# The first SwiGLU products of a decoder trunk: another order of the seven products, and weight sums made earlier

## The chip, the cores and the metric

The kernel runs on one core of one Trainium2 chip. The metric is the time of one execution in microseconds (us). The engines have short names: PE is TensorE (PEld its weight loader), DVE is VectorE, ACT is ScalarE, POOL is GpSimd, SP is SyncE, which issues DMAs.

## What is computed

Two layers of a decoder trunk on 512 tokens of width 1024. Each has a SwiGLU block, a mixer and a second SwiGLU block, each followed by a layer norm:

```python
def swiglu(x, w13, w2):
    a, b = jnp.split(x @ w13, 2, axis=-1)
    return (jax.nn.silu(a) * b) @ w2
...
    for l in range(DEPTH):
        x = layer_norm(ALPHA * x + 0.5 * swiglu(x, ffn1_w13[l], ffn1_w2[l]), ln_g[l, 0], ln_b[l, 0])
        m = mixer(x, w_in[l], ...)
        x = layer_norm(ALPHA * x + m, ln_g[l, 1], ln_b[l, 1])
        x = layer_norm(ALPHA * x + 0.5 * swiglu(x, ffn2_w13[l], ffn2_w2[l]), ln_g[l, 2], ln_b[l, 2])
```

The inner width of a SwiGLU is 2816, so `w13` has 22 column blocks of 128 for `a` and 22 for `b`. All data are float32. The change touches only `x @ w13`, in the four SwiGLU blocks.

## The kernel before

**Split numbers.** A float32 operand is split into a high and a low part (`split`, L126 and L127): ScalarE copies the source into a reduced type (`h_...`, the high part), and VectorE subtracts that copy from the source (`l_...`, the low part). A product is then three matmuls: high by high, high by low, low by high. So each split is a ScalarE instruction followed by a VectorE instruction that waits for it.

**Seven products instead of eight.** In `seven_pairs` two column blocks `k` and `k + 11` are taken together; with `a` and `b` that gives a two-by-two block product of the weights' quarters with the quarters of `x`. It is computed with seven products instead of eight, in which sums of quarters take the place of quarters. There are ten such pairs in a SwiGLU block (an eleventh is computed plainly first). The weights' quarters of a pair are four tiles `a`, `b`, `c`, `d` of 128x1024, loaded by SyncE (`load`, L553); four sums are made of them in place on VectorE (`sum`, L570): `t = a + b`, `b = d + b`, `a = a + b` (with the new `b`), `c = a + c` (with the new `a`). The sums of `x` are `s1` to `s4`.

**The order of the work** is written out by hand. The table `ORDER` has a row for each of the seven products: the bank of PSUM that it is added up in (`X`, `A`, or `C`, which is two banks wide), the part of `x`, and the weight tile:

```python
    ORDER = (("X", "A11", "a"), ("C", "s1", "t"), ("X", "s2", "a"), ("C", "s4", "d"), ("X", "s3", "b"),
             ("A", "A12", "c"), ("X", "A22", "c"))
    AHEAD = 3
```

The loop over `n` makes one product a step (`m` is the step in the pair, 0 to 6). In each step it issues, in this order: the evictions of the product before (`evictions`), a weight sum in the steps that have one, the split of the weights that are needed `AHEAD` = 3 steps later, and the product itself (`product` L603; `wide` L589 and L591 for bank C). The evictions bring a product out of PSUM: copies and Silu on ScalarE, adds and multiplications on VectorE. A tile that is used raw first and as a sum later (`a` is used in products one and three, `c` in six and seven) is split, summed, and split again.

In six of the ten pairs (`due`: pairs 1, 2, 4, 5, 7 and 8) the loop also calls `activation_sums` (L337 to L341, and splits) for an earlier pair's result, which the output product needs later; in three of them two DMAs (L348) then store the result.

What runs on VectorE, ScalarE and SyncE in this stage is kept in program order (`pin`). TensorE's instructions are ordered by the scheduler: it puts some matmuls of the next pair's first product ahead of this pair's last ones, since they go to another bank. POOL meanwhile adds up weight sums of the output product in DRAM by DMA (L307).

The buffers: four of `a` and `b` (two pairs' worth), two each of `c` and `d`, one of `t`, and five pairs of high and low parts. A load waits until the last reader of its buffer is done.

Of the kernel before, what the change touches and what calls it, by code (L numbers as in the profile page):

```python
# [31 lines left out]
AF = mybir.ActivationFunctionType  # L32
ALU = mybir.AluOpType
# [50 lines left out]
def trunk(ctx: ExitStack, tc, x_in, xt_in, w13, w2, w_in, w_iv, w_br, w_out, ln_g, ln_b, lb_in, hgn, sgg, sgb, sgws,  # L84
          sgbs, masks, tril_in, ident_in, out):
    nc = tc.nc
    V, S, G, PE = nc.vector, nc.scalar, nc.gpsimd, nc.tensor
# [9 lines left out]
    def bank(name):  # L97
        return psum.tile([P, 512], F32, tag="ps", name=name)
# [21 lines left out]
    def pin(ins):  # L120

        if pinned[0]:
            tc.keep_in_program_order(ins)

    def split(hi, lo, src):
        pin(S.activation(hi, src, AF.Copy))  # L126
        pin(V.tensor_tensor(lo, src, hi.bitcast(F32), op=ALU.subtract))  # L127
# [371 lines left out]
    def x_sums(s, gap=X_GAP):  # L499
# [26 lines left out]
        for q in range(2):  # L526
# [2 lines left out]
        parts("s4")  # L529


    ORDER = (("X", "A11", "a"), ("C", "s1", "t"), ("X", "s2", "a"), ("C", "s4", "d"), ("X", "s3", "b"),
             ("A", "A12", "c"), ("X", "A22", "c"))
    AHEAD = 3

    class PairWeights:
# [25 lines left out]
        def split(self):  # L562
            src = ORDER[len(self.parts)][2]
            hi, lo = (wk.tile([P, 2, 512], F32R, tag="w", name=f"{v}_p{src}_{self.k}", bufs=NW) for v in "hl")
# [7 lines left out]
    def seven_pairs(seven, s, ks, weights_of, first, due):  # L572


        half = slice(0, 256), slice(256, 512)
        movs = {"A11": lambda m: (xh[m // 2][:, m % 2, half[0]], xl[m // 2][:, m % 2, half[0]]),
                "A12": lambda m: (xh[2 + m // 2][:, m % 2, half[0]], xl[2 + m // 2][:, m % 2, half[0]]),
                "A22": lambda m: (xh[2 + m // 2][:, m % 2, half[1]], xl[2 + m // 2][:, m % 2, half[1]])}
        for c in s:
            movs[c] = lambda m, c=c: tuple(s[c][m // 2][:, m % 2, z] for z in range(2))  # L580

        def wide(ps, units, c, first):

            for z in range(2):
                hi, lo = units[0][:, z], units[1][:, z]
                for m in range(4):
                    ms = slice(m * P, (m + 1) * P)
                    v = s[c][m // 2][:, m % 2]
                    PE.matmul(ps[z][:, 0:256], lo[:, ms], v[:, 0], start=first and m == 0, stop=False,  # L589
                              skip_group_check=True)  # L590
                    PE.matmul(ps[z], hi[:, ms], v.rearrange("p z t -> p (z t)"), start=False, stop=(m == 3),  # L591
                              skip_group_check=True)
                    flow.tick(120.0 + 227.0)

        def product(ps, units, c, first):
            for z in range(2):
                hi, lo = units[0][:, z], units[1][:, z]
                for m in range(4):
                    ms = slice(m * P, (m + 1) * P)
                    mh, ml = movs[c](m)  # L600
                    for i, (a, v) in enumerate(((hi, mh), (hi, ml), (lo, mh))):
                        start = first and z == 0 and m == 0 and i == 0
                        PE.matmul(ps[:, half[z]], a[:, ms], v, start=start, stop=(m == 3 and i == 2),  # L603
                                  skip_group_check=not (first and z == 0))
                    flow.tick(3 * 120.0)

        pws = {ks[0]: first}
        at = lambda n: (ks[n // 7], n % 7)
        last = 7 * len(ks)
        banks = {}  # L610

        def evictions(k, m):

            b, r = banks[k], seven.room(k)
            X, C, A = b["X"].rearrange("p (z t) -> p z t", z=2), b["C"], b["A"].rearrange("p (z t) -> p z t", z=2)
            c12, c22 = r[:, 0:2], r[:, 2:4]
            if m == 0:
                b["c11"] = wk.tile([P, 2, 256], F32, tag="sa", name="c11", bufs=NSA)
                pin(S.activation(b["c11"], X, AF.Copy))  # L619
            elif m == 1:  # L620
                for z in range(2):
                    pin(S.activation(c22[:, z], C[z][:, 256:512], AF.Copy))
                for z in range(2):
                    pin(V.tensor_tensor(c22[:, z], c22[:, z], C[z][:, 0:256], op=ALU.add))
            elif m == 2:
                pin(S.activation(c12, X, AF.Copy))
            elif m == 3:
                for z in range(2):
                    for y in range(2):
                        pin(V.tensor_tensor(c12[:, y], C[y][:, 256 * z:256 * z + 256], c12[:, y],  # L630
                                            op=ALU.add if z else ALU.subtract))
            elif m == 4:
                pin(V.tensor_tensor(c22, c22, X, op=ALU.subtract))
            elif m == 5:
                pin(V.tensor_tensor(b["c11"], b["c11"], A, op=ALU.add))
                yield
                pin(S.activation(b["c11"], b["c11"], AF.Silu))
                pin(V.tensor_tensor(c12, c12, b["c11"], op=ALU.mult))
            elif m == 6:
                c21 = wk.tile([P, 2, 256], F32, tag="sa", name="c21", bufs=NSA)  # L640
                pin(S.activation(c21, X, AF.Silu))
                yield
                pin(V.tensor_tensor(c22, c22, c21, op=ALU.mult))

        for n in range(last):
            k, m = at(n)
            nk = at(n + 7)[0] if n + 7 < last else None
            if m == 0 and nk is not None:
                pws[nk] = weights_of(nk)
                pws[nk].load_d()  # L650
            elif m == 1 and nk is not None:
                pws[nk].load_c()
            ev = evictions(*at(n - 1)) if n else iter(())
            next(ev, None)
            if m == 0:
                banks[k] = {"X": bank(f"fX{k}"), "C": [bank(f"fC{k}{z}") for z in range(2)], "A": bank(f"fA{k}")}
            elif m == 3:
                pws[k].sum("c", "a", "c")
            elif m == 4 and nk is not None:
                pws[nk].sum("t", "a", "b")  # L660
            elif m == 5 and nk is not None:
                pws[nk].sum("b", "d", "b")
            elif m == 6 and nk is not None:
                pws[nk].sum("a", "a", "b")
            if n + AHEAD < last:
                pws[at(n + AHEAD)[0]].split()
            for _ in ev:
                pass
            if m == 3:
                for v in due.get(k, ()):  # L670
                    seven.activation_sums(v)
            c, mov, _ = ORDER[m]
            (wide if c == "C" else product)(banks[k][c], pws[k].parts[m], mov, m in (0, 1, 5))
        for _ in evictions(*at(last - 1)):
            pass

# [7 lines left out]
    def ffn(l, i, first, next_weights):  # L684
# [82 lines left out]
        in_dram = flow.add(seven.sums_in_dram(order))  # L767
        pinned[0] = True
        seven_pairs(seven, s, by_seven, weights_of, pw, dict(zip((1, 2, 4, 5, 7, 8), ([v] for v in front + by_seven[0:5]))))
        pinned[0] = False  # L770
        flow.finish(in_dram)
# [538 lines left out]
```

## Time and profile before

| | us |
|---|---|
| three runs | 2087.88, 2093.77, 2092.84 (median 2092.84) |
| the profiled execution | 2091.45 |
| its span, from the first to the last instruction | 2089.7 |
| the four stages of `seven_pairs`, from their first to their last matmul | 213.2, 216.7, 215.6, 216.6 |

The stages take 862 us together, about two fifths of the span. The profile names an instruction by its line, engine, operation and tiles: `l_pa<-ra,h_pa` is the low part of `a`'s split, made from the raw tile `ra` and the high part `h_pa`. `fX`, `fA` and `fC` are the banks, `xh` and `xl` the parts of `x`, `xs` the split sums of `x`, `r` the result of a pair, `c` at L637 or L641 the tiles `c11` and `c21`. In rows of time the first number is the start in us from the span's start, the second the duration; in square brackets stands how long the engine was idle before, and for whom. Instructions of one engine overlap a little: the time from start to start is shorter than the duration.

### The profile page before, as it was taken

How to read it: one execution, taken by the hardware profiler on the slowest of the kernel's cores; microseconds unless marked ns; L12 is line 12 of the kernel's file. 1: busy time of each engine (PE TensorE's matmuls, PEld its weight loads, DVE VectorE, ACT ScalarE, POOL GpSimd, SP SyncE). 2: the span in 40 equal slices, each digit the busy share in tenths (PEclk: the TensorE clock that was granted, in tenths of full speed). 3: DMA queues.
4: the chain of work that ended last, by engine and by line, in shares of the span. 5: the costliest groups of instructions: out<-in, count | busy, mean ns of one | idle time of the engine just before them, and what ended most of it. 6: DMA issues, size and time to landing. Idle time of an engine off the chain costs nothing. (4 is left out here: it accounts for less than half of the span.)

```text
span 2089.7 us, 32071 instructions
## 1 busy us (share of the span) xinstructions
PE 2035.9 (97%) x12240; PEld 1818.3 (87%) x12240; DVE 1645.0 (79%) x2573; ACT 1010.5 (48%) x1518; POOL 336.3 (16%) x478
## 2 busy tenths in 40 slices
PE   9999999999999999999999999999999999999998
PEld 8889888888888989998899898888888889899886
DVE  8888988956446788889788889889564468888896
ACT  5545565335323545456554455653353235444563
POOL 1322002301000122200113310032010001232001
PEclk9999999999999999999999999999999999999999
DMA  7998676735243399867669986776352434998573
GB/s 244 253 258 205 215 249 226 167 111 172 91 141 112 136 262 232 210 192 261 208 173 244 256 205 211 258 243 132 123 170 84 154 105 144 268 234 229 167 264 132
DMA packets 167546, 404.52 MB, mean 194 GB/s; under 512 B 18880, under 2 KB 19008, under 8 KB 167392
## 3 DMA queue, kind: packets, MB, share of 16 engines
q1 hardware_dynamic: 113472, 261.22, 37.3%
q0 software_dynamic: 53920, 141.26, 28.2%
q8 instruction: 96, 1.57, 0.3%
q14 instruction: 58, 0.48, 0.1%
HBM read 380.38 MB, written 131.07 MB: 245 GB/s over the span
## 5 line engine op out<-in xcount | busy, mean ns | idle before, releaser
L307 POOL DMA_DIRECT2D t<-in_w_dram x176 | 145.3, 892 | 195.4 <-DMA t<-in_w_dram 102.6
L126 ACT ACTIVATE h_pa<-ra 128x1024 fp32r<-128x1024 f32 x80 | 84.1, 1052 | 181.6 <-DVE ra L570 181.6
L127 DVE TENSOR_TENSOR l_pc<-rc,h_pc 128x1024 fp32r<-128x1024 f32 x80 | 97.9, 1224 | 47.2 <-ACT h_pc L126 47.2
L127 DVE TENSOR_TENSOR l_pa<-ra,h_pa 128x1024 fp32r<-128x1024 f32 x80 | 97.8, 1223 | 43.4 <-ACT h_pa L126 43.4
L603 PE MATMUL fX<-xh,l_pa 128*128 128x256 f32 x320 | 93.7, 293 | 38.5 <-DVE l_pa L127 38.5
L603 PE MATMUL fX<-xs,h_pa 128*128 128x256 f32 x640 | 117.1, 283 | 1.6 <-ACT c L619 1.6
L603 PE MATMUL fX<-xs,h_pb 128*128 128x256 f32 x640 | 116.7, 283 | 0.0
L591 PE MATMUL fC<-xs,h_pd 128*128 128x512 f32 x320 | 115.0, 399 | 0.0
L591 PE MATMUL fC<-xs,h_pt 128*128 128x512 f32 x320 | 114.7, 398 | 0.0
L126 ACT ACTIVATE h_pc<-rc 128x1024 fp32r<-128x1024 f32 x80 | 85.2, 1065 | 50.1 <-DVE rc L570 50.1
L603 PEld LDWEIGHTS fX<-xs,h_pa 128*128 128x128 f32 x640 | 102.0, 191 | 4.2 <-ACT c L619 2.6
L603 PEld LDWEIGHTS fX<-xs,h_pb 128*128 128x128 f32 x640 | 102.3, 191 | 2.1
L307 POOL DMA_DIRECT2D t<-t x104 | 56.4, 542 | 292.1 <-DMA t<-in_w_dram 259.7
L155 PE MATMUL z<-xh,h_z 128*128 128x512 f32 x256 | 103.1, 403 | 0.0
L155 PE MATMUL z<-xh,l_z 128*128 128x512 f32 x256 | 99.9, 390 | 0.0
L155 PE MATMUL z<-xl,h_z 128*128 128x512 f32 x256 | 99.8, 390 | 0.0
L603 PEld LDWEIGHTS fX<-xh,l_pa 128*128 128x128 f32 x320 | 61.8, 193 | 43.3 <-DVE l_pa L127 43.3
L603 PE MATMUL fX<-xh,h_pc 128*128 128x256 f32 x320 | 94.7, 296 | 0.0
L603 PE MATMUL fX<-xh,l_pc 128*128 128x256 f32 x320 | 94.6, 296 | 0.0
L603 PE MATMUL fX<-xl,h_pc 128*128 128x256 f32 x320 | 94.5, 295 | 0.0
L589 PE MATMUL fC<-xs,l_pt 128*128 128x256 f32 x320 | 90.2, 282 | 1.5 <-DVE l_pt L127 1.5
L603 PE MATMUL fX<-xl,h_pa 128*128 128x256 f32 x320 | 91.4, 286 | 0.0
(391 smaller groups left out, 6970.6 us busy)
## 6 DMA issues: line engine op xcount, KB each, us to landing
t<-in_w_dram POOLq DMA_DIRECT2D x88, 512.0 KB, 10.1
t<-t POOLq DMA_DIRECT2D x104, 256.0 KB, 5.0
r_d<-t SPq DMA_DIRECT2D x104, 256.0 KB, 4.0
t<-in_w_dram POOLq DMA_DIRECT2D x88, 256.0 KB, 6.5
r_c<-in_w_dram SPq DMA_DIRECT2D x44, 512.0 KB, 4.9
ra<-in_w_dram SPq DMA_DIRECT2D x80, 256.0 KB, 6.3
rb<-in_w_dram SPq DMA_DIRECT2D x80, 256.0 KB, 7.6
rc<-in_w_dram SPq DMA_DIRECT2D x80, 256.0 KB, 10.3
```

The costliest lines, as they stand in the source:

```text
L126: pin(S.activation(hi, src, AF.Copy))
L127: pin(V.tensor_tensor(lo, src, hi.bitcast(F32), op=ALU.subtract))
L155: PE.matmul(ps[:, n0:n0 + n], a[:, cs], m[:, n0:n0 + n], start=(i == 0), stop=(i == 3 * nk - 1))
L307: tc.keep_in_program_order(nc.gpsimd.dma_start(*of(k), **kw))
L589: PE.matmul(ps[z][:, 0:256], lo[:, ms], v[:, 0], start=first and m == 0, stop=False, skip_group_check=True)
L591: PE.matmul(ps[z], hi[:, ms], v.rearrange("p z t -> p (z t)"), start=False, stop=(m == 3), skip_group_check=True)
L603: PE.matmul(ps[:, half[z]], a[:, ms], v, start=start, stop=(m == 3 and i == 2), skip_group_check=not (first and z == 0))
```

## The change

The diff has three parts. `ORDER` is permuted: the product with `A12` and raw `c` (bank A) goes from sixth to second place, the one with `s1` and `t` (bank C) from second to fourth, the one with `s4` and `d` (bank C) from fourth to sixth; products one, three, five and seven stay. The evictions are renumbered accordingly, and the final multiplication of `c12` now follows the second product out of bank C. The sums are made in other steps, and behind the step's split and evictions instead of ahead of the split. The activation sums go from step 3 to step 1.

```diff
-    ORDER = (("X", "A11", "a"), ("C", "s1", "t"), ("X", "s2", "a"), ("C", "s4", "d"), ("X", "s3", "b"),
-             ("A", "A12", "c"), ("X", "A22", "c"))
+    ORDER = (("X", "A11", "a"), ("A", "A12", "c"), ("X", "s2", "a"), ("C", "s1", "t"), ("X", "s3", "b"),
+             ("C", "s4", "d"), ("X", "A22", "c"))
...
             elif m == 1:
+                pin(V.tensor_tensor(b["c11"], b["c11"], A, op=ALU.add))
+                yield
+                pin(S.activation(b["c11"], b["c11"], AF.Silu))
+            elif m == 2:
+                pin(S.activation(c12, X, AF.Copy))
+            elif m == 3:
                 for z in range(2):
                     pin(S.activation(c22[:, z], C[z][:, 256:512], AF.Copy))
                 for z in range(2):
                     pin(V.tensor_tensor(c22[:, z], c22[:, z], C[z][:, 0:256], op=ALU.add))
-            elif m == 2:
-                pin(S.activation(c12, X, AF.Copy))
-            elif m == 3:
+            elif m == 4:
+                pin(V.tensor_tensor(c22, c22, X, op=ALU.subtract))
+            elif m == 5:
                 for z in range(2):
                     for y in range(2):
                         pin(V.tensor_tensor(c12[:, y], C[y][:, 256 * z:256 * z + 256], c12[:, y],
                                             op=ALU.add if z else ALU.subtract))
-            elif m == 4:
-                pin(V.tensor_tensor(c22, c22, X, op=ALU.subtract))
-            elif m == 5:
-                pin(V.tensor_tensor(b["c11"], b["c11"], A, op=ALU.add))
-                yield
-                pin(S.activation(b["c11"], b["c11"], AF.Silu))
                 pin(V.tensor_tensor(c12, c12, b["c11"], op=ALU.mult))
...
-            elif m == 3:
-                pws[k].sum("c", "a", "c")
-            elif m == 4 and nk is not None:
-                pws[nk].sum("t", "a", "b")
-            elif m == 5 and nk is not None:
-                pws[nk].sum("b", "d", "b")
-            elif m == 6 and nk is not None:
-                pws[nk].sum("a", "a", "b")
             if n + AHEAD < last:
                 pws[at(n + AHEAD)[0]].split()
             for _ in ev:
                 pass
-            if m == 3:
+            if m == 0:
+                pws[k].sum("c", "a", "c")
+            elif m == 3 and nk is not None:
+                pws[nk].sum("t", "a", "b")
+            elif m == 4 and nk is not None:
+                pws[nk].sum("b", "d", "b")
+            elif m == 5 and nk is not None:
+                pws[nk].sum("a", "a", "b")
+            if m == 1:
                 for v in due.get(k, ()):
                     seven.activation_sums(v)
             c, mov, _ = ORDER[m]
-            (wide if c == "C" else product)(banks[k][c], pws[k].parts[m], mov, m in (0, 1, 5))
+            (wide if c == "C" else product)(banks[k][c], pws[k].parts[m], mov, m in (0, 1, 3))
```

No instruction is added or taken away; what moves is seen in the engines' rows. VectorE in the kernel before, from the third pair's sum `ra` to its sum `rc` (L570 are the sums, L127 the subtractions of the splits, the rest are evictions):

```order
L570 TENSOR_TENSOR ra_578<-ra_578,rb_579 128x1024
L127 TENSOR_TENSOR l_pa_791<-ra_578,h_pa_790 128x1024
L638 TENSOR_TENSOR r_627<-r_627,c_628 128x512
L127 TENSOR_TENSOR l_pd_836<-rd_584,h_pd_835 128x1024
L643 TENSOR_TENSOR r_627<-r_627,c_829 128x512
L127 TENSOR_TENSOR l_pb_870<-rb_579,h_pb_869 128x1024
L624 TENSOR_TENSOR r_866<-r_866,fC_832 128x256
L624 TENSOR_TENSOR r_866<-r_866,fC_833 128x256
L127 TENSOR_TENSOR l_pc_897<-rc_259,h_pc_896 128x1024
L570 TENSOR_TENSOR rc_259<-ra_578,rc_259 128x1024
L127 TENSOR_TENSOR l_pc_927<-rc_259,h_pc_926 128x1024
```

The same sums of the same pair on VectorE in the changed kernel:

```order
L570 TENSOR_TENSOR ra_578<-ra_578,rb_579 128x1024
L636 TENSOR_TENSOR r_628<-fC_590,r_628 128x256
L636 TENSOR_TENSOR r_628<-fC_591,r_628 128x256
L636 TENSOR_TENSOR r_628<-fC_590,r_628 128x256
L636 TENSOR_TENSOR r_628<-fC_591,r_628 128x256
L638 TENSOR_TENSOR r_628<-r_628,c_629 128x512
L127 TENSOR_TENSOR l_pa_793<-ra_578,h_pa_792 128x1024
L127 TENSOR_TENSOR l_pt_836<-rt,h_pt_835 128x1024
L643 TENSOR_TENSOR r_628<-r_628,c_829 128x512
L570 TENSOR_TENSOR rc_259<-ra_578,rc_259 128x1024
L127 TENSOR_TENSOR l_pb_871<-rb_579,h_pb_870 128x1024
```

Before, the subtraction `l_pa` and the second `l_pc` stand right behind the sums `ra` and `rc` that they read; now five evictions stand between `ra` and `l_pa`, and the second `l_pc` has moved out of the piece, to two steps later.

ScalarE in the kernel before, from the third pair's first split of `c` on (`r<-fX` is the copy `c12` out of bank X, `th` belongs to the activation sums):

```order
L126 ACTIVATE h_pc_896<-rc_259 128x1024
L626 ACTIVATE r_866<-fX_831 128x512
L126 ACTIVATE h_pc_926<-rc_259 128x1024
L126 ACTIVATE th_931<-r_400 128x256
L126 ACTIVATE th_931<-s_930 128x512
L126 ACTIVATE h_pa_965<-ra_820 128x1024
```

ScalarE in the changed kernel, from the third pair's activation sums to the copies out of bank C (L623 is the Silu of `c11`, L625 the copy `c12`):

```order
L126 ACTIVATE th_875<-r_401 128x256
L126 ACTIVATE th_875<-s_874 128x512
L126 ACTIVATE h_pd_913<-rd_584 128x1024
L623 ACTIVATE c_868<-c_868 128x512
L625 ACTIVATE r_867<-fX_831 128x512
L126 ACTIVATE h_pc_943<-rc_259 128x1024
L628 ACTIVATE r_867<-fC_832 128x256
L628 ACTIVATE r_867<-fC_833 128x256
```

The Silu of `c11`, which stood near the pair's end, now stands behind the activation sums and ahead of the copy `c12`, the split of `c` and the copies out of bank C. On SyncE the loads keep their order in the stage; at its end three loads of `r_b` (L378) have moved ahead of six fetches of stored activation sums (L356). POOL's instructions keep their order.

## The prediction

> **What bounds the kernel now.** I read the clock and span first, then the busy shares, then who waits for whom on TensorE, then the order of time on TensorE and VectorE inside the stage that the change touches.
>
> ```profile
> core 0: 2089.7 us, clock 0.993
> PE 2035.9 (97%) x12240; PEld 1818.3 (87%) x12240; DVE 1645.0 (79%) x2573; ACT 1010.5 (48%) x1518; POOL 336.3 (16%) x478
> ```
>
> TensorE works nearly all the time, so only two things can get shorter: its idle time and its slowed time. Its waits, and those of its weight loader, name the place:
>
> ```profile
> PE fX L603 <- DVE l_pa L127: 38.5, 24, 2.0
> PE pA L366 <- DVE l_b L127: 1.0, 2, 0.7
> ...
> PEld fX L603 <- DVE l_pa L127: 43.3, 24, 2.2
> ```
>
> The columns are the total in us, the number of waits and the longest one. Nearly all idle time is one kind: a product of the first SwiGLU stage waits for the low part `l_pa` of a weight that VectorE is still subtracting. There are 24 such waits: four feed-forward stages with six pairs each. In the code `due` names exactly six pairs (1, 2, 4, 5, 7, 8) in which VectorE also makes activation sums; I call them loaded pairs. TensorE in order of time, first the start of the second product in three pairs that follow each other, then one wait:
>
> ```profile
> 73.90 0.28 PE L589 MATMUL fC<-xs,l_pt 128*128 128x256 f32 x1
> ...
> 96.17 0.28 PE L589 MATMUL fC<-xs,l_pt 128*128 128x256 f32 x1
> ...
> 116.22 0.28 PE L589 MATMUL fC<-xs,l_pt 128*128 128x256 f32 x1
> ```
>
> ```profile
> 88.31 0.28 PE L603 MATMUL fX<-xl,h_pa 128*128 128x256 f32 x1
> 90.55 0.39 PE L603 MATMUL fX<-xh,l_pa 128*128 128x256 f32 x1 [1.96 <-DVE l_pa L127]
> 90.77 0.28 PE L603 MATMUL fX<-xh,h_pa 128*128 128x256 f32 x1
> 90.89 0.28 PE L603 MATMUL fX<-xl,h_pa 128*128 128x256 f32 x1
> ```
>
> A pair without a wait takes 116.22 - 96.17 = 20.05 us, which is TensorE's own work; the pair before took 22.27. Matmuls start every 0.12 us, so the gap of 2.24 us cost about 2.1. The same stretch on VectorE shows why:
>
> ```profile
> 71.61 1.22 DVE L570 TENSOR_TENSOR ra<-ra,rb 128x1024 f32<-128x1024 f32 x1
> 74.04 1.23 DVE L127 TENSOR_TENSOR l_pa<-ra,h_pa 128x1024 fp32r<-128x1024 f32 x1 [1.21 <-ACT h_pa L126]
> 75.19 0.69 DVE L638 TENSOR_TENSOR r<-r,c 128x512 f32<-128x512 f32 x1
> 76.00 1.23 DVE L127 TENSOR_TENSOR l_pd<-rd,h_pd 128x1024 fp32r<-128x1024 f32 x1
> ...
> 79.53 1.22 DVE L127 TENSOR_TENSOR l_pc<-rc,h_pc 128x1024 fp32r<-128x1024 f32 x1
> 80.79 1.23 DVE L570 TENSOR_TENSOR rc<-ra,rc 128x1024 f32<-128x1024 f32 x1
> 83.14 1.23 DVE L127 TENSOR_TENSOR l_pc<-rc,h_pc 128x1024 fp32r<-128x1024 f32 x1 [1.13 <-ACT h_pc L126]
> 84.28 0.42 DVE L337 TENSOR_TENSOR s<-r 128x256 f32<-128x256 f32 x1
> ...
> 86.81 1.41 DVE L630 TENSOR_TENSOR r<-fC,r 128x256 f32<-128x256 f32 x4
> 88.14 1.22 DVE L570 TENSOR_TENSOR rt<-ra,rb 128x1024 f32<-128x1024 f32 x1
> 89.27 1.22 DVE L127 TENSOR_TENSOR l_pa<-ra,h_pa 128x1024 fp32r<-128x1024 f32 x1
> ...
> 93.87 1.22 DVE L570 TENSOR_TENSOR ra<-ra,rb 128x1024 f32<-128x1024 f32 x1
> ...
> 113.60 1.22 DVE L570 TENSOR_TENSOR ra<-ra,rb 128x1024 f32<-128x1024 f32 x1
> ```
>
> From `ra` to `ra` VectorE needs 93.87 - 71.61 = 22.26 us in a loaded pair and 113.60 - 93.87 = 19.73 in the next. The loaded pair is VectorE's length, not TensorE's: **VectorE sets the pace there**. Twice in a pair it stands still, because it makes a weight sum and the very next thing is to split that sum: ScalarE must first copy it, and VectorE waits (1.21 and 1.13).
>
> The slowed time stands in the same stages. The first and the last of seven stretches that the trace shows at half clock, each 3.41 us long (the next to last column is the DMA share, the one before it the granted clock), and TensorE at the first:
>
> ```profile
> 781.65:785.06 3.41, 3.41 (x18) 3.41 (x17) 3.41 (x5) 0.00 (x0) 0.56 (x1) 0.50 1.10 228
> ...
> 1952.42:1955.83 3.41, 3.41 (x18) 3.41 (x17) 3.03 (x4) 0.27 (x1) 0.00 (x0) 0.50 0.42 129
> ```
>
> ```profile
> 779.10 0.28 PE L603 MATMUL fX<-xl,h_pa 128*128 128x256 f32 x1
> 781.34 0.39 PE L603 MATMUL fX<-xh,l_pa 128*128 128x256 f32 x1 [1.96 <-DVE l_pa L127]
> ...
> 781.69 0.41 PE L603 MATMUL fX<-xl,h_pa 128*128 128x256 f32 x1
> 781.90 0.41 PE L603 MATMUL fX<-xh,l_pa 128*128 128x256 f32 x1
> ```
>
> A wait ends at 781.34, and at 781.65 the clock is 0.50 for 3.41 us. Matmuls then start every 0.21 us instead of 0.12, so 3.41 / 0.21 = 16 start in the stretch, and it costs 3.41 - 16 x 0.12 = 1.5 us.
>
> The Trainium skill ("TensorE: Matmul & The Clock Gate", Part 1: The HAM clock gate) says that the gate falls back to half after at least one idle window of about 3.4 us. A gap of 2.24 us fills no such window, so by that rule the waits would not be what halves the clock, the stretches would stay and the sum would be 2052; the trace speaks against it, as the drop stands right behind the gap.
>
> **The change part by part.**
>
> *What goes.* Both standstills go: the sum `ra` now stands five VectorE instructions ahead of its split, and `rc` three products ahead. If VectorE keeps up, all 24 waits go. The loader's row is nearest to the loss: 43.3 us, plus 24 x 0.07 because a load lasts 0.19 and the next starts after 0.12 (the matmul's 0.28 against 0.12, on 38.5, gives 42.4): **45.0 us**. With the waits I let the seven half-clock stretches go: 7 x 1.5 = 10.4. Together 55.4.
>
> *What VectorE needs now.* No instruction is added or taken away, so I add up starts from the rows. Seven subtractions at 1.14 (89.27 is such a one) are 7.97; four sums at 1.13 (88.14 to 89.27) 4.53; four 512-wide evictions at 0.60 are 2.40; six 256-wide ones at 0.33 (86.81 to 88.14 for four) 2.0; activation sums 86.81 - 84.28 = 2.53. That is 19.4. It agrees with before: 22.26 less 1.30 and 1.22 (the two standstills over a start-to-start of 1.13), 0.21 before `l_pd` and 0.12 before `rc` is 19.41.
>
> *The wait that is added.* `c11` is now finished in the third step instead of the seventh. ScalarE's order there becomes Silu of `c11`, copy of `c12`, copy `h_pc`; the first waits for VectorE's add, and VectorE's `l_pc` waits for the third. Behind that Silu are queued the copy that frees bank X for the fifth product, `h_pc`, and the two copies out of bank C. The pieces:
>
> ```profile
> 72.95 1.06 ACT L126 ACTIVATE h_pa<-ra 128x1024 fp32r<-128x1024 f32 x1 [4.70 <-DVE ra L570]
> 73.92 0.61 ACT L637 ACTIVATE c<-c 128x512 f32<-128x512 f32 x1
> 74.44 0.58 ACT L641 ACTIVATE c<-fX 128x512 f32<-128x512 f32 x1
> 74.91 1.05 ACT L126 ACTIVATE h_pd<-rd 128x1024 fp32r<-128x1024 f32 x1
> ```
>
> VectorE's add 0.69, Silu 0.52, copy 0.47 (starts), `h_pc` 1.06 whole: 2.74, and 0.1 for the handings-over (71.61 + 1.22 to 72.95 is 0.12). In that time VectorE does the add's 0.60 and `l_pd`'s 1.14. So it stands 1.1 us, in every pair. Bounds: nothing, if the add comes early enough, and 2.5, the two standstills of before again. I take 1.1, a sum of rows of the same instructions.
>
> So a loaded pair costs VectorE 19.4 + 1.1 = 20.5, against TensorE's 20.05: 0.45 too much, at most 24 x 0.45 = 10.8 us of waits that stay. A pair without activation sums costs it 20.5 - 2.53 = 18.0; three pairs together, 18.0 + 2 x 20.5 = 59.0, fit into 3 x 20.05 = 60.15. Only how far VectorE can run ahead decides. It cannot evict a product before TensorE has made it, so its lead is a step (2.88) less the evictions themselves, more than one loaded pair's 0.45 and perhaps less than what two need together with the start of the stage. Ends 0 and 10.8; I take the middle, **5.4**.
>
> *The moved evictions.* Bank C is written by products four and six, bank X by one, three, five and seven; one step of 2.88 us stands between, as before. Two copies (at most 0.47 each, the start of the wider one above) and two adds (0.33 each) must empty C in it: 1.6 us hide behind product five. If VectorE is late, the wait shows there, on the sixth product. I price it within the 0 to 10.8.
>
> *The moved DMAs.* SyncE's loads follow when buffers come free. `a` comes free three steps earlier, `b` when it did, `d` two steps later, and the two stores of the activation sums, which stand between them on SyncE, go two steps earlier. The tight one is `c`: its first split is now for the second product, not the sixth, four steps earlier.
>
> ```profile
> 69.38 1.88 SPq L553 DMA_DIRECT2D rc<-in_w_dram  x2
> ...
> 100.08 1.07 ACT L126 ACTIVATE h_pc<-rc 128x1024 fp32r<-128x1024 f32 x1
> ```
>
> ```profile
> DMA to landing us min/median/max: 2.6/10.3/15.5
> ```
>
> The load has 30.7 us now, and 30.7 - 4 x 2.88 = 19.2 then, against 15.5 at worst (the row is that of `rc`): hidden, with 3.7 to spare. POOL's transfers keep their order. In a stage the DMA share is 0.84:
>
> ```profile
> 28.84:242.00 213.16, 202.16 (x1522) 193.52 (x1521) 189.12 (x251) 103.83 (x146) 49.35 (x67) 1.00 0.84 223
> ```
>
> With the same bytes in some 13 us less it becomes 0.84 x 213 / 200 = 0.89: still under one. At the end of a stage three loads of `r_b` now stand ahead of six fetches of activation sums; they matter to the 1.0 us on `pA`. Nothing counted, 3 us either way kept for the range, which covers the first products' waits at a stage's start too.
>
> **Sum**, against the profiled execution's 2091.45 us (the median of the runs is 2092.84, 1.4 above it): 2091.45 - 45.0 - 10.4 + 5.4 = **2041.5 us**.
>
> **The rivals.**
>
> *The clock still drops.* If the half-clock stretches come from something else than the waits, 10.4 us stay: 2052. For it: waits of the same length in the first stage show no drop (the row above has a clock of 1.00 over the whole stage, and the wait at 88.31 lies in it). Against it: the drop shown starts 0.31 us after a wait ends, and the other six follow such a wait too. 0.10. This is also what the Trainium skill's rule ("TensorE: Matmul & The Clock Gate", Part 1: The HAM clock gate) comes to here.
>
> *VectorE still sets the pace.* If a second standstill of 1.2 opens (say at the copies out of C), a loaded pair costs 21.7 and loses 1.65: 24 x 1.65 = 40, and half the drops stay, 5: 2091.45 - 55.4 + 45 = 2081. For it: ScalarE and VectorE hand over in both directions at several steps. Against it: ScalarE is busy 48%. 0.10.
>
> *Slower: bank C is handed over late.* If the adds out of C are late in every pair, not only the loaded ones, TensorE stands before product six 40 times. With a sum and a subtraction queued ahead of them (1.13 + 1.14 = 2.27 late) that is 91 us, less the 55.4: 2127. It decides from 55.4 / 40 = 1.4 us per pair. Against it: a pair without activation sums has 2 us to spare on VectorE. 0.04.
>
> *It does not do what it says.* The sums move, but the split's copy on ScalarE is held up by its own queue, and the pair stays 22.3: 2091. Against it: ScalarE waits 4.70 us for `ra` in the row above, it is not late itself. 0.03.
>
> **How the numbers follow.** The forecast has 0.73; its own range is 2091.45 - 55.4 - 3 = 2033 to 2036 + 10.8 = 2047. With the first rival, whose range ends 10.4 later, it is 0.83: I give 2033 to 2057. A measurement of this kernel tells about 0.3%, 6 us. Faster by more: 0.73 + 0.10 + 0.10 = 0.93; within: 0.03; slower: 0.04.
>
> **What would show it.** In the profile after, the row of TensorE waiting for `l_pa` should be gone or under 3 us. What is left should stand on `fC<-h_pd` or `fX<-h_pb`, waiting for VectorE's adds or ScalarE's `c12`, under 11 us. VectorE's wait for `h_pa` should be gone, and its wait for `h_pc` stay at about 1.1 a pair. The clock should be 0.99 to 1.00 with no half-clock stretch in the four stages. The prediction is wrong if 24 waits remain under another name, if the drops stay without waits, or if `rc` makes ScalarE wait for a DMA.

## The result, and the profile after

Each kernel ran four times. Before took a median of 2093.31 us (2087.88 to 2095.37), the changed kernel 2040.09 (2039.76 to 2041.08). The ratio is 0.975, with a 95% interval of 0.9732 to 0.9769: 53 us or 2.5% faster, and 1.4 us from the forecast of 2041.5. The profiled execution took 2041.08.

The page of the kernel after, span, clock and busy shares:

```profile
core 0: 2039.3 us, clock 0.999
PE 2021.2 (99%) x12240; PEld 1806.4 (89%) x12240; DVE 1638.6 (80%) x2573; ACT 1012.7 (50%) x1518; POOL 336.6 (17%) x478
```

The span fell by 50.4 us (2089.7 to 2039.3) with the same number of instructions on every engine. TensorE's busy time fell by 14.7 although it executes the same matmuls. The seven half-clock stretches at 1.5 us each are 10.4 of that (the mean granted clock rose from 0.993 to 0.999); the long tails of the matmuls ahead of the 24 waits, 0.28 us where 0.12 is enough, are another 3.8. The rest of the span's gain is idle time that went.

Who waits for whom on TensorE and its loader in the kernel after (total in us, number, longest):

```profile
PE fX L603 <- ACT c L619: 2.3, 3, 0.8
PE fC L589 <- DVE r L630: 2.0, 7, 0.3
...
PEld fC L589 <- DVE r L630: 4.1, 9, 0.5
```

The row of `l_pa`, 38.5 us in 24 waits before, is gone, and no other row takes its place. What is left in the four stages is of two kinds: a few waits of under a microsecond at the starts of stages, and some short ones before the sixth product, the second into bank C.

The windows of the first and the last stage in the kernel after (length; busy time of PE, PEld, DVE, ACT and POOL with their counts; granted clock; DMA share; GB/s):

```profile
28.83:230.79 201.96, 201.36 (x1522) 193.30 (x1521) 188.06 (x252) 104.61 (x146) 49.34 (x67) 1.00 0.87 238
...
1722.73:1925.57 202.84, 201.63 (x1523) 193.39 (x1522) 189.18 (x253) 105.28 (x147) 48.44 (x67) 1.00 0.87 237
```

The four stages take 201.96, 202.84, 204.25 and 202.84 us, 811.89 together; before they took 862.09. The difference, 50.2, is nearly all of the span's gain of 50.4. The clock is 1.00 in them and none of the seven half-clock stretches is left. The DMA share of the first stage rose from 0.84 to 0.87.

VectorE in the kernel after, over a loaded pair (from `ra` to `ra`) and into the next:

```profile
68.28 1.22 DVE L570 TENSOR_TENSOR ra<-ra,rb 128x1024 f32<-128x1024 f32 x1
69.41 1.41 DVE L636 TENSOR_TENSOR r<-fC,r 128x256 f32<-128x256 f32 x4
70.86 0.69 DVE L638 TENSOR_TENSOR r<-r,c 128x512 f32<-128x512 f32 x1
71.47 1.22 DVE L127 TENSOR_TENSOR l_pa<-ra,h_pa 128x1024 fp32r<-128x1024 f32 x1
...
81.95 1.23 DVE L127 TENSOR_TENSOR l_pc<-rc,h_pc 128x1024 fp32r<-128x1024 f32 x1 [0.99 <-ACT h_pc L126]
...
88.89 1.22 DVE L570 TENSOR_TENSOR ra<-ra,rb 128x1024 f32<-128x1024 f32 x1
...
100.69 1.23 DVE L127 TENSOR_TENSOR l_pc<-rc,h_pc 128x1024 fp32r<-128x1024 f32 x1 [1.64 <-ACT h_pc L126]
...
107.62 1.22 DVE L570 TENSOR_TENSOR ra<-ra,rb 128x1024 f32<-128x1024 f32 x1
```

The bracket behind `l_pa`, 1.21 before, is gone: 3.19 us and five evictions lie between `ra` and its subtraction. `l_pc` waits, 0.99 in the loaded pair and 1.64 in the next. The loaded pair takes 88.89 - 68.28 = 20.61 us and the next 107.62 - 88.89 = 18.73, where it was 22.26 and 19.73.

### The profile page after: what moved, and what is told of

The parts are those of the page before. It is cut to its first block, busy times and chain, and to the rows that moved or that the text cites. A ratio compares the mean times of both kernels' runs of the same rounds, so it can differ in the third digit from the quotient of the medians.

```text
span 2039.3 us, 32166 instructions
## 1 busy us (share of the span) xinstructions
PE 2021.2 (99%) x12240; PEld 1806.4 (89%) x12240; DVE 1638.6 (80%) x2573; ACT 1012.7 (50%) x1518; POOL 336.6 (17%) x478
## 5 line engine op out<-in xcount | busy, mean ns | idle before, releaser
L127 DVE TENSOR_TENSOR l_pc<-rc,h_pc 128x1024 fp32r<-128x1024 f32 x80 | 97.9, 1224 | 47.7 <-ACT h_pc L126 47.7
L127 DVE TENSOR_TENSOR l_pa<-ra,h_pa 128x1024 fp32r<-128x1024 f32 x80 | 97.6, 1220 | 0.0
L127 DVE TENSOR_TENSOR l_b<-r_b,h_b 128x1024 fp32r<-128x1024 f32 (+1 forms) x61 | 73.7, 1210 | 24.5 <-ACT h_b L126 24.3
L589 PE MATMUL fC<-xs,l_pd 128*128 128x256 f32 x320 | 91.0, 284 | 2.3 <-DVE r L630 2.0
L603 PE MATMUL fA<-xh,l_pc 128*128 128x256 f32 x320 | 90.9, 284 | 0.7 <-DVE l_pc L127 0.7
L603 PE MATMUL fX<-xs,l_pa 128*128 128x256 f32 x320 | 90.6, 283 | 0.0
L603 PE MATMUL fA<-xh,h_pc 128*128 128x256 f32 x320 | 90.5, 283 | 0.0
L603 PE MATMUL fA<-xl,h_pc 128*128 128x256 f32 x320 | 90.5, 283 | 0.0
L603 PE MATMUL fX<-xh,h_pc 128*128 128x256 f32 x320 | 90.5, 283 | 0.0
```

## The experiments

Each run stood beside the kernel before on the same chip; its ratio is to that. Medians and changes to before, in us:

| kernel | median | change |
|---|---|---|
| the changed kernel | 2040.09 | -53.2 |
| the changed kernel again, beside the runs marked * | 2039.06 | -53.3 |
| new order, sums in their old places | 2094.38 | +2.9 |
| old order, three sums earlier | 2068.77 | -22.8 |
| the change with the activation sums in their old step * | 2069.24 | -23.1 |
| the same, with the split ahead of a copy | 2035.81 | -57.3 |
| the change with the Silu later * | 2033.99 | -58.4 |
| the change with work added in the loaded pairs | 2099.50 | +8.0 |
| the change with work added in the other pairs * | 2064.27 | -28.1 |
| before, with TensorE's order fixed | 2097.80 | +6.3 |

### The new order with the old places of the sums

Against the changed kernel, the four sums go back to where the kernel before makes them, right ahead of the split:

```diff
             if m == 0:
                 banks[k] = {"X": bank(f"fX{k}"), "C": [bank(f"fC{k}{z}") for z in range(2)], "A": bank(f"fA{k}")}
-            if n + AHEAD < last:
-                pws[at(n + AHEAD)[0]].split()
-            for _ in ev:
-                pass
-            if m == 0:
+            elif m == 3:
                 pws[k].sum("c", "a", "c")
-            elif m == 3 and nk is not None:
+            elif m == 4 and nk is not None:
                 pws[nk].sum("t", "a", "b")
-            elif m == 4 and nk is not None:
+            elif m == 5 and nk is not None:
                 pws[nk].sum("b", "d", "b")
-            elif m == 5 and nk is not None:
+            elif m == 6 and nk is not None:
                 pws[nk].sum("a", "a", "b")
+            if n + AHEAD < last:
+                pws[at(n + AHEAD)[0]].split()
+            for _ in ev:
+                pass
```

> The changed kernel's order of products, but the four weight sums stand where they stood before, right ahead of their splits. Theory 1 (the standstill of VectorE between a sum and its split is what cost the time, and the new order only makes room for earlier sums): both standstills come back, the one at c merges with the new wait behind c11, so a loaded pair costs VectorE 19.4 + 1.2 + 1.2 + 0.2 = 22.0 us against TensorE's 20.05; 24 x 1.95 = 47 us of waits and some half-clock stretches (0 to 10 us): 2088 us, 2080 to 2098. Rival (the new order of products itself gives the time, for instance because the low part of a is asked for later): 2040 to 2046.

Measured: 2094.38 us against 2091.53, ratio 1.0013 (1.0004 to 1.0023). VectorE over a loaded pair of this kernel:

```profile
61.68 1.22 DVE L570 TENSOR_TENSOR rc<-ra,rc 128x1024 f32<-128x1024 f32 x1
...
64.08 1.23 DVE L127 TENSOR_TENSOR l_pc<-rc,h_pc 128x1024 fp32r<-128x1024 f32 x1 [1.18 <-ACT h_pc L126]
...
75.50 1.23 DVE L127 TENSOR_TENSOR l_pa<-ra,h_pa 128x1024 fp32r<-128x1024 f32 x1 [1.21 <-ACT h_pa L126]
...
84.08 1.22 DVE L570 TENSOR_TENSOR rc<-ra,rc 128x1024 f32<-128x1024 f32 x1
```

Both brackets are back at their old size, and the pair takes 84.08 - 61.68 = 22.40 us. So the new order of the products gives nothing by itself, even with the activation sums in their new step; it only makes room for `rc` to be made earlier. The waits of TensorE's weight loader in the same kernel:

```profile
PEld fX L603 <- ACT r L625: 25.2, 24, 1.1
PEld fX L603 <- ACT h_pa L126: 20.1, 24, 0.8
PEld fX L603 <- ACT c L619: 11.7, 28, 1.0
```

The loss is now spread over two waits in each loaded pair and some more between, none over 1.1 us, and no half-clock stretch stands in the stages. It is as large as before all the same: these rows make 57.0 us. Before, the loader's 43.3 on `l_pa`, its 2.6 on the copy of L619 and the 10.4 of the half-clock stretches made 56.3.

### The earlier sums in the old order

Against the kernel before, three of the four sums are made one step earlier and behind the split. The sum `rc` can't go: in the old order a product still needs raw `c`.

```diff
             elif m == 3:
                 pws[k].sum("c", "a", "c")
-            elif m == 4 and nk is not None:
-                pws[nk].sum("t", "a", "b")
-            elif m == 5 and nk is not None:
-                pws[nk].sum("b", "d", "b")
-            elif m == 6 and nk is not None:
-                pws[nk].sum("a", "a", "b")
             if n + AHEAD < last:
                 pws[at(n + AHEAD)[0]].split()
             for _ in ev:
                 pass
+            if m == 3 and nk is not None:
+                pws[nk].sum("t", "a", "b")
+            elif m == 4 and nk is not None:
+                pws[nk].sum("b", "d", "b")
+            elif m == 5 and nk is not None:
+                pws[nk].sum("a", "a", "b")
```

> The order of products of before, with the sums t, b and a made one step earlier and behind the step's split; the sum c cannot go earlier in that order, since raw c is split one step before. Theory 1: the standstill at a goes, the one at c stays; a loaded pair costs VectorE 22.26 - 1.3 to 1.5 = 20.9 us, 0.85 over TensorE's 20.05: 24 x 0.85 = 20 us stay of 55: about 2058 us, 2050 to 2066, with VectorE's wait for h_pa gone and that for h_pc as before. Rival (the order of products gives the time): no gain, 2085 to 2094.

Measured: 2068.77 us, ratio 0.9893 (0.9878 to 0.9908), 3 us above the expected range. VectorE in a loaded pair of this kernel:

```profile
71.14 1.22 DVE L570 TENSOR_TENSOR ra<-ra,rb 128x1024 f32<-128x1024 f32 x1
72.28 0.68 DVE L635 TENSOR_TENSOR c<-c,fA 128x512 f32<-128x512 f32 x1
73.57 1.23 DVE L127 TENSOR_TENSOR l_pa<-ra,h_pa 128x1024 fp32r<-128x1024 f32 x1 [0.61 <-ACT h_pa L126]
...
82.67 1.23 DVE L127 TENSOR_TENSOR l_pc<-rc,h_pc 128x1024 fp32r<-128x1024 f32 x1 [1.13 <-ACT h_pc L126]
```

The theory was right in kind and wrong in size. In the old order only one short eviction falls between `ra` and `l_pa`, so that standstill is halved (1.21 to 0.61) and not removed; the one at `rc` is whole. TensorE's row and the first stage's window:

```profile
PE fX L603 <- DVE l_pa L127: 26.1, 24, 1.4
```

```profile
29.80:238.50 208.70, 202.24 (x1522) 193.52 (x1521) 189.27 (x251) 103.48 (x145) 49.37 (x67) 1.00 0.84 227
```

The same 24 waits are there as before, of 1.4 us at most instead of 2.0, and the clock is 1.00 in all four stages. So the half-clock stretches hang on the length of the waits, not on their being there alone.

### The changed kernel with the activation sums in their old step

```diff
-            if m == 1:
+            if m == 3:
                 for v in due.get(k, ()):
                     seven.activation_sums(v)
```

> The changed kernel with the activation sums back in the fourth step, where they stood before. Theory 1 (only VectorE's length of a pair counts, and its lead of about a step): no change beyond 4 us, 2036 to 2044. Rival (moving the activation sums away from the split of c was part of the gain): 2050 or more.

Measured: 2069.24 us against 2092.37, ratio 0.9893 (0.9878 to 0.9908). The theory missed by 25 us, and the rival was right. The prediction had given this part of the diff no price at all; 30 of the 53 us depend on it. TensorE's wait, then ScalarE, VectorE and TensorE in a loaded pair of this kernel:

```profile
PE fC L589 <- DVE r L630: 28.7, 25, 1.2
```

```profile
79.49 0.60 ACT L625 ACTIVATE r<-fX 128x512 f32<-128x512 f32 x1 [0.71 <-PE fX L603]
79.98 1.05 ACT L126 ACTIVATE h_pc<-rc 128x1024 fp32r<-128x1024 f32 x1
```

```profile
81.07 1.23 DVE L127 TENSOR_TENSOR l_pc<-rc,h_pc 128x1024 fp32r<-128x1024 f32 x1 [1.82 <-ACT h_pc L126]
...
83.35 0.42 DVE L337 TENSOR_TENSOR s<-r 128x256 f32<-128x256 f32 x1
...
85.88 0.75 DVE L630 TENSOR_TENSOR r<-r,fC 128x256 f32<-128x256 f32 x2
```

```profile
86.34 0.39 PE L589 MATMUL fC<-xs,l_pd 128*128 128x256 f32 x1 [1.19 <-DVE r L630]
```

Read it from the top. The copy `c12` (L625) waits for TensorE's third product. The copy `h_pc` stands behind it in ScalarE's queue, and `l_pc` on VectorE waits for that copy. So VectorE cannot run ahead of TensorE over this point: it is tied to it once per pair. Behind the tie stand `l_pc`, `rt`, the activation sums (2.53 us) and the adds of L630, which empty bank C; before the sixth product may start, all that must be done. From the copy at 79.49 to the sixth product at 86.34 it takes 6.85 us, where TensorE works two products, four and five, of 2.88 at most. With the activation sums two steps earlier they stand ahead of the tie, where VectorE has time.

The length of a pair on VectorE did not show this. Leaving its waits aside, it has the same work per pair in both kernels.

### The same, with the split ahead of the copy

If the tie is the cause, it should be enough to take it away. The kernel of the last experiment gets one `yield`, which puts the copy `c12` behind the step's split on ScalarE:

```diff
             elif m == 2:
+                yield
                 pin(S.activation(c12, X, AF.Copy))
...
-            if m == 1:
+            if m == 3:
                 for v in due.get(k, ()):
                     seven.activation_sums(v)
```

> The kernel with the activation sums back in the fourth step (2069 us), and ScalarE's split of c now ahead of its copy c12 out of bank X. New theory (what counts is the work on VectorE between the point where it is tied to TensorE, here the copy c12 behind the third product, on which the split of c and so all that follows is queued, and the point where TensorE needs its result, the adds out of bank C ahead of the sixth product): without the copy in front the split of c starts some 1.3 us earlier, the activation sums run in time that was idle, and the waits of 1.35 us go: 2036 to 2046. Rival (activation sums right ahead of the adds delay them in any case): 2064 to 2070.

Measured: 2035.81 us against 2093.14, ratio 0.9738 (0.9715 to 0.9761), 0.2 us under the expected range. ScalarE and VectorE in a loaded pair of this kernel:

```profile
77.15 1.04 ACT L126 ACTIVATE h_pc<-rc 128x1024 fp32r<-128x1024 f32 x1
78.34 0.60 ACT L626 ACTIVATE r<-fX 128x512 f32<-128x512 f32 x1 [0.15 <-PE fX L603]
```

```profile
78.22 1.23 DVE L127 TENSOR_TENSOR l_pc<-rc,h_pc 128x1024 fp32r<-128x1024 f32 x1 [0.51 <-ACT h_pc L126]
...
83.03 0.74 DVE L631 TENSOR_TENSOR r<-r,fC 128x256 f32<-128x256 f32 x2
```

`h_pc` no longer waits for TensorE, and VectorE reaches the adds out of bank C 83.03 - 78.34 = 4.69 us after the copy `c12` starts, against 85.88 - 79.49 = 6.39 in the kernel before it. The activation sums stand in their old step, and yet 33 us come back. So it was the tie, not the step of the activation sums as such.

### The Silu later

In the changed kernel `h_pc` also stands behind the Silu of `c11`, which waits for VectorE's add: the wait that the prediction said was added. The Silu is put off by three steps:

```diff
             elif m == 1:
                 pin(V.tensor_tensor(b["c11"], b["c11"], A, op=ALU.add))
-                yield
-                pin(S.activation(b["c11"], b["c11"], AF.Silu))
...
             elif m == 4:
                 pin(V.tensor_tensor(c22, c22, X, op=ALU.subtract))
+                yield
+                pin(S.activation(b["c11"], b["c11"], AF.Silu))
```

> The changed kernel with the Silu of c11 put off from the third step to the sixth, behind that step's split on ScalarE. Theory 1 (what is left of the waits comes from the chain c11, Silu, copy c12, split of c, on which VectorE stands 1.0 to 1.1 us a pair): the standstill goes, a loaded pair costs VectorE 19.5 us, less than TensorE's 20.05, TensorE's wait for the adds out of bank C (4.1 us on its weight loader) goes: 2034 to 2038. Rival (VectorE is no longer what the rest waits for): 2040, no change.

Measured: 2033.99 us, ratio 0.9725 (0.971 to 0.9739), beside the changed kernel's 2039.06 on the same chip: 5 us less, and the two ranges (2033.64 to 2034.17, and 2038.35 to 2040.71) do not touch. The same place on VectorE, in a loaded pair:

```profile
78.04 1.22 DVE L127 TENSOR_TENSOR l_pd<-rd,h_pd 128x1024 fp32r<-128x1024 f32 x1
79.18 1.23 DVE L127 TENSOR_TENSOR l_pc<-rc,h_pc 128x1024 fp32r<-128x1024 f32 x1
```

The bracket behind `l_pc` is gone, and with it the waits for L630 on TensorE. This is the fastest kernel of the study. It and the moved copy of the experiment before were not tried together.

### Work added to VectorE, in the loaded pairs and in the others

Four reductions, 0.60 us each from start to start, are added to VectorE in the second step: in one kernel in the six loaded pairs, in another in the other four (there with `k not in due`). Nothing reads their result.

```diff
+            if m == 1 and k in due:
+                for _ in range(4):
+                    pin(V.tensor_reduce(small("dm", 4), pws[k].b[:, 0].rearrange("p (t c) -> p t c", t=4),
+                                        axis=AX.X, op=ALU.add))
```

In the loaded pairs:

> The changed kernel with four reductions (0.6 us each, 2.4 in all, their result is not used) added on VectorE in the second step of the six loaded pairs. Theory 1 (VectorE's length of a loaded pair sets TensorE's pace there, one for one, and waits of 2 us make half-clock stretches): 24 x 2.4 = 58 us more and 0 to 10 for the clock, 2095 to 2110, with half-clock stretches back in the stages. Rival (VectorE has room, the time came from elsewhere): under 2050. Rival on the clock (the half-clock stretches do not come from the waits): waits of 2 us are back and the clock stays at full in the stages.

Measured: 2099.5 us, ratio 1.0034 (1.0018 to 1.0049). Over the changed kernel that is 59 us. Four half-clock stretches, 6 us, are in it; the other 53 are 53 / 24 = 2.2 for each loaded pair, where 4 x 0.60 = 2.4 were added. VectorE has next to nothing to spare in these pairs. TensorE's wait, its row in time, and the half-clock stretch behind it:

```profile
PE fX L603 <- ACT r L625: 41.4, 24, 2.2
```

```profile
84.78 0.40 PE L591 MATMUL fC<-xs,h_pt 128*128 128x512 f32 x1
...
86.96 0.50 PE L603 MATMUL fX<-xs,h_pb 128*128 128x256 f32 x2 [1.78 <-ACT r L625]
```

```profile
87.58:90.99 3.41, 3.41 (x19) 3.41 (x18) 3.10 (x5) 2.71 (x5) 1.02 (x1) 0.50 0.97 192
```

With waits of that length four half-clock stretches are back, in a kernel that has none without the reductions.

In the other pairs:

> The changed kernel with the same four reductions (2.4 us, result not used) added on VectorE in the other four pairs of each stage. Theory 1: those pairs then cost VectorE 18.0 + 2.4 = 20.4 us and give back no lead; a stage's ten pairs are 4 x 20.4 + 6 x 20.5 = 205 us against TensorE's 200.5, of which about 1 us was lost before: 3 to 4 us more in each stage, about 2054, 2044 to 2058. Rival (each pair by itself, no lead is carried over): 16 x 0.35 = 6 us more, 2046. Rival (VectorE does not matter): 2040.

Measured: 2064.27 us, ratio 0.987 (0.9853 to 0.9886), 6 us above the expected range. VectorE's `ra` at the start of such a pair, of the loaded pair behind it and of the next:

```profile
91.51 1.22 DVE L570 TENSOR_TENSOR ra<-ra,rb 128x1024 f32<-128x1024 f32 x1
...
111.98 1.22 DVE L570 TENSOR_TENSOR ra<-ra,rb 128x1024 f32<-128x1024 f32 x1
...
132.59 1.22 DVE L570 TENSOR_TENSOR ra<-ra,rb 128x1024 f32<-128x1024 f32 x1
```

The lengthened pair takes 111.98 - 91.51 = 20.47 us, the loaded one 132.59 - 111.98 = 20.61: all pairs are now longer than TensorE's 20.05. The loader's waits in this kernel:

```profile
PEld fC L589 <- DVE r L630: 16.4, 35, 0.5
PEld fX L603 <- ACT r L625: 7.6, 4, 2.3
```

Together they are 24.0 us, where the changed kernel has 4.1. The first row has grown by 12.3, about the 3 to 4 us in each stage that the expectation had worked out from the lengths of the pairs, and these came out as expected (20.47 and 20.61 for 20.4 and 20.5). A pair of 18.73 gives back the lead that the loaded pairs behind it use up; without it nearly all of the forty pairs wait a little before the sixth product. The rival without a lead, 2046, falls.

What the expectation had at nothing is the second row. In the first pair of each stage VectorE has no lead yet, and with the added work TensorE waits once before the fifth product. The longest of the four waits, 1.99 us up to 1069.35, is followed by a half-clock stretch, the only one in this kernel:

```profile
1070.15:1073.56 3.41, 3.41 (x18) 3.41 (x17) 3.28 (x5) 2.53 (x5) 0.00 (x0) 0.50 1.07 202
```

The 7.6 and the stretch's 1.5 are 9.1 us, about what the run lies above the expected 2054.

### TensorE's order fixed in the kernel before

Was the loss before a matter of the order in which the matmuls stand on TensorE? In the kernel before, the matmuls of the stage are pinned in program order:

```diff
-                    PE.matmul(ps[z][:, 0:256], lo[:, ms], v[:, 0], start=first and m == 0, stop=False,
-                              skip_group_check=True)
+                    pin(PE.matmul(ps[z][:, 0:256], lo[:, ms], v[:, 0], start=first and m == 0, stop=False,
+                                  skip_group_check=True))
...
-                        PE.matmul(ps[:, half[z]], a[:, ms], v, start=start, stop=(m == 3 and i == 2),
-                                  skip_group_check=not (first and z == 0))
+                        pin(PE.matmul(ps[:, half[z]], a[:, ms], v, start=start, stop=(m == 3 and i == 2),
+                                      skip_group_check=not (first and z == 0)))
```

> The kernel before, with TensorE's matmuls of the stage kept in program order, so that the next pair's first product is no longer begun ahead of product seven. Theory 1: VectorE's length decides, not the moment at which the low part of a is asked for; the later need (24 matmuls, 2.9 us) is won once in each of four stages, at most 12 us: 2078 to 2093. Rival (TensorE asked for the low part of a too early, and that was the wait): 2036 to 2050.

Measured: 2097.8 us, ratio 1.0032 (1.0017 to 1.0047), 5 us above the range of the theory; the rival, a gain of 40 us or more, falls. TensorE's wait and its place in time:

```profile
PE fX L603 <- DVE r L633: 46.0, 28, 2.0
```

```profile
66.45 0.28 PE L603 MATMUL fA<-xh,l_pc 128*128 128x256 f32 x1
68.70 0.35 PE L603 MATMUL fX<-xh,h_pc 128*128 128x256 f32 x1 [1.98 <-DVE r L633]
```

TensorE waits no less than before (38.5 us there), only under another name: for bank X before product seven. The 7.5 us more are about what the kernel is slower. Both standstills of VectorE, 1.21 and 1.13, are there as before; TensorE meets the engine that is behind at another place. That the wait names `l_pa` was thus no proof that `l_pa` was the trouble. The small gain that the theory allowed did not come.

## Why the prediction was right

**What goes.** The step said that both standstills go from the rows of sum and split, and with them 24 waits, 45.0 us. It held: `l_pa` waits for nothing, TensorE's row is gone, and putting the sums back (first experiment) brings both standstills and the whole loss back.

**The clock.** The seven stretches, 10.4 us, were booked as a consequence of the waits. They are gone, and the runs bear out the cause: 24 waits of up to 1.4 us (earlier sums in the old order), 25 of up to 1.2 (late activation sums) and the many of up to 1.1 (late sums) halved no clock, while waits of about 2 us came with four stretches where the loaded pairs had more work, with one where the others had it, and with seven in the pinned kernel, as in the kernel before. The first rival, 2052, falls. So, for this kernel, does the rule behind it in the Trainium skill ("TensorE: Matmul & The Clock Gate", Part 1: The HAM clock gate), as far as it asks for an idle window of about 3.4 us: here 2.2 us from matmul to matmul were enough. That waits of 2 us in the first stage of the kernel before brought no drop, which the prediction set down in that rival's favour, comes from where they lie in time (last section).

**What VectorE needs.** Forecast for a loaded pair 20.5, of which 1.1 was the new wait for `h_pc`; measured 20.61 and, over all 40 pairs:

```profile
DVE l_pc L127 <- ACT h_pc L126: 47.7, 40, 1.7
```

That is 1.2 each. Taking the chain away (the Silu later) gained 5 us, so it was this chain that cost the rest. For the other pairs 18.0 was forecast and 18.73 measured. There VectorE has caught up with TensorE, and its wait for `h_pc` is longer (1.64 in the timeline above); TensorE is not kept waiting by it.

**What stays.** 5.4 us were taken from the middle between 0 and 10.8. What is left is 4.1 us on the loader's row before the sixth product, the place that the prediction had named. TensorE at one of them in the kernel after:

```profile
84.70 0.39 PE L589 MATMUL fC<-xs,l_pd 128*128 128x256 f32 x1 [0.30 <-DVE r L630]
```

The stages lost 50.2 us where the terms gave 50.0. The middle was a choice, not a finding, and that it came so near was luck. The reductions in the other pairs show that VectorE's lead was the right thing to look at: it is gathered in the others and used up in the loaded pairs.

**The moved DMAs.** The load of `c` was to land within 19.2 us. In the kernel after, for `rc`:

```profile
DMA to landing us min/median/max: 3.3/8.3/13.9
```

It is hidden, and no row of ScalarE waits for it. The DMA share came to 0.87, not 0.89.

**What the prediction did not see.** It added up VectorE's instructions per pair and so took it as all one in which step the activation sums stand. That step of it is wrong, and the sum came out right only because the change had moved them. Without the move the same working would have given 2041.5 too, and the kernel takes 2069 (third experiment). What it lacked is the tie: ScalarE's `h_pc` queues behind a copy that waits for TensorE, so the lead does not reach over that point, and the work between the tie and the adds out of bank C has to fit into two products by itself. The prediction had a rival that names this place (bank C handed over late, from 1.4 us per pair) but let it begin in every pair and with other work in the way; with the activation sums late it came in the loaded pairs only, and gave 2069.

## What to carry to other kernels

Where a result goes to another engine and back before the next instruction can use it, put other work of the first engine in between. The total of an engine per round says whether it can keep up; where it can, look for the points at which its queue, or one that it waits for, is tied to the slower engine, and add up what stands between each tie and the next hand-over. When a wait vanishes in one place, look at the next meeting of the same two engines before counting it as gain.

## What the runs showed of the hardware

TensorE's clock fell to half after pauses much shorter than the half-clock stretches themselves. In the kernel with more work in the loaded pairs, 86.96 - 84.78 = 2.18 us from matmul to matmul end 0.62 us ahead of 3.41 us at 0.50; in the pinned kernel 68.70 - 66.45 = 2.25 end 0.85 us ahead of this:

```profile
69.55:72.96 3.41, 3.41 (x18) 3.41 (x18) 3.01 (x4) 0.29 (x1) 0.83 (x1) 0.50 0.95 269
```

Not every such pause was followed by a drop: 24 gave four in the one, 28 gave seven in the other. The traces show most of what decides. Another of the seven stretches in the kernel before:

```profile
846.50:849.91 3.41, 3.41 (x18) 3.41 (x17) 3.41 (x5) 0.00 (x0) 1.15 (x2) 0.50 0.87 305
```

It starts 64.85 us = 19 x 3.413 behind the first, at 781.65, and the last, at 1952.42, starts 1170.77 us = 343 x 3.4133 behind it. All stretches of an execution lie on one grid with steps of 3.413 us, and each fills one step. TensorE's idle time, added up in each step of the four kernels that have such stretches, gives this: all 18 steps with 1.89 us of it or more were followed by a stretch, of the ten with 1.78 to 1.88 one was (the 1.78 shown above, ahead of 87.58), and of those with 1.67 or less none. In the other kernels no 3.41 us between the first matmul and the last hold more than 1.60.

So a pause of 2 us halved the clock where it lay within one step, and not where a border between two steps cut it. The wait of 1.96 us ahead of 90.55 in the kernel before is cut at 781.65 - 203 x 3.4133 = 88.74: 1.80 us are left for the next step, and no drop follows. The wait of the same length ahead of 781.34 lies within one step. Counted from the start of the span, the grid lies elsewhere in each of the four traces. That it also moves between executions of one kernel is not shown, but their mean granted clocks differ: the kernel before ran at 0.997 in 2085.0 us and at 0.989 in 2094.36. The 10.4 us of the prediction are thus those of its profiled execution.
